# Order of the last products of a sum of squares, and a scheduling priority for the casts of streamed weights, in a two-layer decoder trunk

## The chip, the cores and the metric

The kernel runs on one core of a Trainium2 chip. The metric is the device time in microseconds (us) of one execution; the time of a kernel is the median of several.

## The reference, cut to what matters

The input `h` has 256 tokens of 1024 features, in fp32. Each of two layers adds three sub-layers to it: a SwiGLU feed-forward, a mixer (differential attention, an RWKV-7 recurrence and an HGRN2 recurrence side by side, gated and projected), and a second feed-forward. Each sub-layer begins with a normalization over the features:

```python
def rms_norm(x, w, eps=EPS):
    xf = x.astype(jnp.float32)
    y = xf * lax.rsqrt(jnp.mean(xf * xf, axis=-1, keepdims=True) + eps)
    return (y * w.astype(jnp.float32)).astype(x.dtype)
...
    for l in range(DEPTH):
        ...
        u = modulate(rms_norm(h, norm_w[l, 0]), m[0], m[1])
        h = h + 0.5 * m[2] * swiglu(u, ffn_w_gate[l, 0], ffn_w_up[l, 0], ffn_w_down[l, 0])
        u = modulate(rms_norm(h, norm_w[l, 1]), m[3], m[4])
        ...
        h = h + m[5] * y
        u = modulate(rms_norm(h, norm_w[l, 2]), m[6], m[7])
        h = h + 0.5 * m[8] * swiglu(u, ffn_w_gate[l, 1], ffn_w_up[l, 1], ffn_w_down[l, 1])
```

All weights are fp32 in HBM and each is used once.

## The kernel before

`h` lies transposed on chip as eight tiles of 128 features x 256 tokens. The weights come as a stream of 446 items, each a block of 128 x 1024 fp32 (512 KB, some 384 KB). All but the first six go through `load(i)`: SyncE issues the DMA into `raw` (four buffers), and `split(wh, wl, raw)` (L371 to L373) makes two parts of it, `wh`, a rounded copy made by ScalarE (ACT), and `wl = raw - wh`, made by VectorE (DVE). Each of `wh` and `wl` has three buffers. `mm3` (L369) then multiplies an item with activations that are split in the same way (`uh`, `ul`; `hh`, `hl`; `zh`, `zl`; `yh`, `yl`): three products for each block of 128 x 128, 24 for an item, added up in one of four PSUM banks `psd`. Some mixer items are taken the other way round by `tm_proj` (L953 to L955, products of 512 columns).

The stages follow one another as the items do: in each layer 68 items of the first feed-forward (44 gate and up, 24 down), 87 of the mixer (its last eight, `w_out`, add to `h`) and 68 of the second feed-forward. While the projections of a mixer run on TensorE (PE), the recurrences and the attention are worked through in small pieces between the items: on DVE the inversion of triangular matrices (L800 to L820), and for the attention scores (L1195, L1200 to L1204), exponentials `ae` (L1207 on ACT, L1217 on DVE), their transposes (L1222 on PE, copied to `apt` by L1224 on ACT), the products with the values `av` (L1234; `av` is copied out of its banks by L1174 on ACT), squares of the result `aot` (L1240), its transposes (L1252) and the tiles `oa` for the output projection. Gates `g` leave their banks by L1267 on ACT. L750 is a product of RWKV with a tile `BK` from ACT.

**The normalization.** The last items of a stage (down or `w_out`) each finish one tile of `h`. `z_tile` then makes the split tiles `zh`, `zl` of it and calls `z_square`: ACT squares the tile (L417), and GpSimd (POOL) adds the squares of tiles 1 to 6 to that of tile 0 (`acc`, L419). The square of tile 7 stays by itself as `sq`. `z_sums` sums `acc` and `sq` over the features by PE products with ones (L430, two for each, into one bank `psm`), and a chain of small DVE instructions (`nst`, L434 and L377 to L382) takes the inverse root, from which the diagonal `nv` (L437) and, by one more product (L441), `rstd` is made. `z_sums` is called by `z_close`, after the first item of the next stage has been written, with a priority of 584 (`PRIO["z"]`). The next stage begins with products of `zh`, `zl`, which need no `rstd`, and changes to `uh`, `ul` (made by `make_u`, L392) some items later. There are six such normalizations: one at the start, five at a change of stage.

**What sets the order.** A list scheduler orders the instructions of each engine when the kernel is built: of those that it holds ready, that with the highest priority goes first, and priority falls with the place in the program. `ahead(n)` gives the instructions written under it the priority of a place n instructions earlier. On the chip each engine then runs its list in that order, and waits where an operand or a buffer is not ready.

Of the kernel before, what the change touches and what calls it, by code (L numbers as in the profile page):

```python
# [63 lines left out]
def trunk(ctx: ExitStack, tc: tile.TileContext, A, out):  # L64
# [14 lines left out]
    def psm(shape):  # L79
        return pm.tile(shape, F32, name="psm", tag="psm")  # L80
# [176 lines left out]
    NOW = {}  # L257
# [8 lines left out]
    def ahead(n):  # L266
        return tc.high_priority(n) if n else nullcontext()
# [103 lines left out]
    def split(dst_h, dst_l, src):  # L371
        SC.copy(dst_h, src)  # L372
        V.tensor_sub(dst_l, src, dst_h.bitcast(F32))  # L373


    def rsqrt_few(y, v, t):
        V.tensor_scalar(y.bitcast(I32), v.bitcast(I32), 1, None, ALU.logical_shift_right)  # L377
        V.tensor_scalar(y.bitcast(I32), y.bitcast(I32), -1.0, float(0x5F3759DF), ALU.mult, ALU.add)
        for _ in range(3):
            V.scalar_tensor_tensor(t, v, -0.5, y, ALU.mult, ALU.mult)  # L380
            V.tensor_mul(t, t, y)
            V.scalar_tensor_tensor(y, t, 1.5, y, ALU.add, ALU.mult)  # L382
# [39 lines left out]
    def z_close():  # L422
        with ahead(PRIO["z"]):
            z_sums()

    def z_sums():
        ps = psm([128, 2])
        for i, sq in enumerate((NOW["acc"], NOW["sq"])):
            for b in range(2):
                PE.matmul(ps[:, b:b + 1], sq[:, b * 128:(b + 1) * 128], ones[:, 0:1],  # L430
                          start=i + b == 0, stop=i + b == 2)
        st = NOW["st"] = tp.tile([128, 3, 2], F32, name="nst", tag="nst", bufs=1)
        dg = NOW["dg"] = tp.tile([128, 2, 128], F32, name="nv", tag="nv", bufs=1)
        V.tensor_scalar(st[:, 0], ps, 1.0 / D, EPS, ALU.mult, ALU.add)  # L434
        rsqrt_few(st[:, 1], st[:, 0], st[:, 2])
        for b in range(2):
            V.tensor_scalar(dg[:, b], ident, st[:, 1, b:b + 1], None, ALU.mult)  # L437
# [901 lines left out]
    def load(i):  # L1339
        src, n, fn, b = items[i]  # L1340
        raw = wp.tile([128, n], F32, name="raw", tag="raw", bufs=RAWB)
        nc.sync.dma_start(raw, src)
        wh = wp.tile([128, n], F32R, name="wh", tag="wh", bufs=WHB)
        wl = wp.tile([128, n], F32R, name="wl", tag="wl", bufs=WLB)
        split(wh, wl, raw)
        return wh, wl, fn, b

    live = deque()
# [13 lines left out]
    for t in range(KT):  # L1362
# [7 lines left out]
        if t < NI:  # L1370
            raw = NOW["ff"].tile([128, D], F32, name=f"raw{t}")
# [12 lines left out]
    for i in range(NI, len(items) + AHEAD):  # L1384
        if i < len(items):
            live.append(load(i))
        while len(live) > (AHEAD if i < len(items) else len(items) + AHEAD - 1 - i):
            wh, wl, fn, b = live.popleft()
            advance(b)
            fn(wh, wl)  # L1390
# [80 lines left out]
```

## Time and profile before

| | before |
|---|---|
| median of 3 runs | 1454.53 us (1451.75 to 1456.83) |
| the profiled execution | 1448.06 us, span 1446.4 us |
| PE matmuls busy | 1397.5 us (97%) |
| PE weight loads busy (PEld) | 1325.0 us (92%) |
| DVE busy | 1185.8 us (82%) |
| ACT busy | 804.4 us (56%) |
| POOL busy | 149.0 us (10%) |
| mean granted clock of PE | 0.992 of full speed |

The shares are of the span. PE appears twice: a product first loads 128 x 128 of one operand (PEld), and the matmul proper then streams the other; the two overlap. The profile is of one execution, which was shorter than the median of the three timed ones.

### The profile page before, as it was taken

The numbers are of one execution on the slowest core, as the hardware profiler recorded it, in microseconds if no ns is written. First come the engines' busy times: TensorE is split into PE (matmuls) and PEld (weight loads), VectorE is DVE, ScalarE is ACT, GpSimd is POOL, SyncE is SP. The second block draws the span as 40 slices with busy tenths as digits, with TensorE's granted clock in tenths as the row PEclk, the third lists the DMA queues.
The fourth block names the chain that finished last, engine by engine and source line by source line (L and its number), as shares of the span: only waits on it lengthen the run. The fifth ranks groups of instructions, "written<-read, shape, count | busy, mean of one in ns | idle before, by whom it ended". The sixth has DMA issues, their size and how long they took to land. (4 is left out here: it accounts for less than half of the span.)

```text
span 1446.4 us, 31230 instructions
## 1 busy us (share of the span) xinstructions
PE 1397.5 (97%) x12424; PEld 1325.0 (92%) x12424; DVE 1185.8 (82%) x2216; ACT 804.4 (56%) x1375; POOL 149.0 (10%) x251
## 2 busy tenths in 40 slices
PE   4999999999899999999999999999989999999998
PEld 2899999998778999999999999999877889999998
DVE  5899988869779999888879888787797787886553
ACT  3565457874255646554555554588534664565542
POOL 6100010031310021000100000100322001100000
PEclk9999999999799999999999999999999999999999
DMA  9679985445416657899878998644552235665664
GB/s 334 247 267 359 341 303 167 148 155 163 137 61 191 203 190 265 298 330 319 297 255 292 353 347 294 194 141 142 180 162 83 88 129 175 198 220 194 193 197 124
DMA packets 90212, 315.99 MB, mean 218 GB/s; under 512 B 10577, under 2 KB 13009, under 8 KB 90066
## 3 DMA queue, kind: packets, MB, share of 16 engines
q1 hardware_dynamic: 86690, 308.32, 63.0%
q0 software_dynamic: 1600, 4.20, 1.2%
q8 instruction: 97, 1.59, 0.4%
q10 hardware_dynamic: 1776, 1.48, 0.3%
q14 instruction: 49, 0.40, 0.1%
HBM read 311.86 MB, written 2.10 MB: 217 GB/s over the span
## 5 line engine op out<-in xcount | busy, mean ns | idle before, releaser
L372 ACT CAST wh<-raw 128x1024 fp32r<-128x1024 f32 (+1 forms) x440 | 455.9, 1036 | 427.4 <-PE psd L369 241.5
L373 DVE TENSOR_TENSOR wl<-raw,wh 128x1024 fp32r<-128x1024 f32 (+1 forms) x440 | 537.2, 1222 | 109.1 <-ACT wh L372 106.2
L369 PE MATMUL psd<-uh,wl 128*128 128x256 f32 x1664 | 227.5, 278 | 6.2 <-DVE wl L373 6.2
L369 PE MATMUL psd<-uh,wh 128*128 128x256 f32 x1664 | 230.8, 280 | 0.0
L369 PE MATMUL psd<-ul,wh 128*128 128x256 f32 x1664 | 226.6, 278 | 0.0
L369 PEld LDWEIGHTS psd<-uh,wl 128*128 128x128 f32 x1664 | 206.0, 188 | 7.9 <-DVE wl L373 7.4
L369 PEld LDWEIGHTS psd<-uh,wh 128*128 128x128 f32 x1664 | 207.2, 188 | 5.0 <-issue 2.6
L369 PEld LDWEIGHTS psd<-ul,wh 128*128 128x128 f32 x1664 | 206.0, 188 | 0.4
L321 DVE SCALAR_TENSOR_TENSOR mw<-mw,cbc 128x1024 f32<-128x1024 f32 x134 | 168.0, 1256 | 0.0
L369 PE MATMUL psd<-hl,wh 128*128 128x256 f32 x704 | 96.0, 277 | 0.0
L369 PE MATMUL psd<-hh,wl 128*128 128x256 f32 x704 | 95.9, 277 | 0.0
L369 PE MATMUL psd<-hh,wh 128*128 128x256 f32 x704 | 95.5, 276 | 0.0
L419 POOL TENSOR_TENSOR acc<-acc,sq 128x256 f32<-128x256 f32 x36 | 31.4, 873 | 573.2 <-ACT sq L417 572.9
L369 PEld LDWEIGHTS psd<-hh,wl 128*128 128x128 f32 x704 | 87.2, 188 | 0.0
L369 PEld LDWEIGHTS psd<-hl,wh 128*128 128x128 f32 x704 | 87.2, 188 | 0.0
L369 PEld LDWEIGHTS psd<-hh,wh 128*128 128x128 f32 x704 | 87.0, 188 | 0.0
L954 PE MATMUL psd<-wl,uh 128*128 128x512 f32 x160 | 66.9, 418 | 3.9 <-DVE wl L373 3.8
L955 PE MATMUL psd<-wh,ul 128*128 128x512 f32 x160 | 67.7, 423 | 0.0
L953 PE MATMUL psd<-wh,uh 128*128 128x512 f32 x160 | 66.4, 416 | 0.0
L369 PE MATMUL psd<-zh,wh 128*128 128x258 f32 x448 | 65.2, 286 | 0.0
L369 PE MATMUL psd<-zh,wl 128*128 128x258 f32 x448 | 64.9, 283 | 0.0
L369 PE MATMUL psd<-zl,wh 128*128 128x258 f32 x448 | 64.0, 283 | 0.0
(430 smaller groups left out, 2032.0 us busy)
## 6 DMA issues: line engine op xcount, KB each, us to landing
raw<-in_gu SPq DMA_DIRECT2D x176, 512.0 KB, 4.7
mw<-in_modw SPq DMA_DIRECT2D x134, 512.0 KB, 5.4
raw<-in_wfm SPq DMA_DIRECT2D x94, 512.0 KB, 3.3
raw<-in_dn SPq DMA_DIRECT2D x64, 512.0 KB, 4.6
raw<-in_wtm SPq DMA_DIRECT2D x40, 512.0 KB, 3.3
raw<-in_dn SPq DMA_DIRECT2D x32, 384.0 KB, 4.1
raw<-in_wo SPq DMA_DIRECT2D x24, 512.0 KB, 3.3
raw<-in_wout SPq DMA_DIRECT2D x16, 512.0 KB, 3.3
```

The costliest lines, as they stand in the source:

```text
L321: ins = V.scalar_tensor_tensor(w, w, 1.0, NOW["cbc"], ALU.mult, ALU.mult, accum_out=modd[:, l, j, f:f + 1])
L369: PE.matmul(p, w[:, sl[k]], xs[k][x], start=first and i == 0, stop=last and i == 3 * n - 1)
L372: SC.copy(dst_h, src)
L373: V.tensor_sub(dst_l, src, dst_h.bitcast(F32))
L419: GP.tensor_add(NOW["acc"], NOW["acc"], sq)
L953: PE.matmul(ps[b], u[k][0][:, ts_], w1, start=k == 0, stop=False)
L954: PE.matmul(ps[b], u[k][0][:, ts_], w2, start=False, stop=False)
L955: PE.matmul(ps[b], u[k][1][:, ts_], w1, start=False, stop=k == KT - 1)
```

## The change

`z_sums` takes the square of the last tile first and the accumulated squares second; `start` and `stop` go by the place in the loop, so the sum is the same. And the two instructions of `split` in `load` are written under `ahead(100)`. From there on every line number is one higher.

```diff
     def z_sums():
         ps = psm([128, 2])
-        for i, sq in enumerate((NOW["acc"], NOW["sq"])):
+        for i, sq in enumerate((NOW["sq"], NOW["acc"])):
             for b in range(2):
                 PE.matmul(ps[:, b:b + 1], sq[:, b * 128:(b + 1) * 128], ones[:, 0:1],
                           start=i + b == 0, stop=i + b == 2)
...
         wh = wp.tile([128, n], F32R, name="wh", tag="wh", bufs=WHB)
         wl = wp.tile([128, n], F32R, name="wl", tag="wl", bufs=WLB)
-        split(wh, wl, raw)
+        with ahead(100):
+            split(wh, wl, raw)
         return wh, wl, fn, b
```

PE at the end of the first mixer, where `w_out` products (`yh`, `yl`) give way to those of the second feed-forward (`zh`, `zl`):

```order
@@ -2832,5 +2838,4 @@
 L369 MATMUL psd<-yl_6721,wh 128x256
 L369 MATMUL psd<-yl_6746,wh 128x256
-L430 MATMUL psm<-ones,acc 128x1 x2
 L369 MATMUL psd<-yl_6765,wh 128x256
 L369 MATMUL psd<-yh_6613,wl 128x256
@@ -2845,4 +2850,5 @@
 L369 MATMUL psd<-zh,wl 128x258 x6
 L430 MATMUL psm<-ones,sq 128x1 x2
+L430 MATMUL psm<-ones,acc 128x1 x2
 L369 MATMUL psd<-zh,wl 128x258
 L369 MATMUL psd<-zl,wh 128x258 x7
```

The two products of `acc` stood in the last `w_out` item, 22 products of weights ahead of those of `sq`; now they stand right behind them. The same happens at all five changes of stage, with 62 to 64 products between the two places where a feed-forward ends.

DVE in the inversion of the first mixer (`TM` and `Y` are its tiles):

```order
 L800 TENSOR_TENSOR TM<-Y,NT 128x392
 L802 TENSOR_REDUCE Y<-TM 128x2x14
+L373 TENSOR_TENSOR wl<-raw,wh 128x1024
 L800 TENSOR_TENSOR TM<-Y,NT 128x450
-L373 TENSOR_TENSOR wl<-raw,wh 128x1024
 L802 TENSOR_REDUCE Y<-TM 128x2x15
 L373 TENSOR_TENSOR wl<-raw,wh 128x1024
```

One `wl` goes ahead of one L800. From the next L802 to the end of the inversion (L809, L812, L814, L817 with a `wl` behind each) DVE's list is the same in both kernels.

ACT in the attention of the second layer, where the most instructions change places:

```order
 L1207 ACTIVATE ae,ast_15161<-psm,ast_15161,ars_14626 128x256 x2
+L372 CAST wh<-raw 128x1024
+L1224 COPY apt<-psm 128x512
+L372 CAST wh<-raw 128x1024 x2
+L1240 ACTIVATE aot,hss<-psm 128x128 x4
+L1224 COPY apt<-psm 128x512
 L1174 COPY av<-psd 128x512
 L372 CAST wh<-raw 128x1024
-L1224 COPY apt<-psm 128x512
-L1267 ACTIVATE g_14671<-psd 128x256
-L1224 COPY apt<-psm 128x512
-L372 CAST wh<-raw 128x1024
```

Three casts, one copy of `apt` and the squares of `aot` now stand ahead of the second copy of `apt` and the second of `av`. In the rest of the attention and of RWKV a small instruction mostly has one cast more ahead of it than before. On PE the matching small products have moved both ways, by up to 20 products of weights later and, in this attention, the first four L1252 by 20 to 25 earlier; between its first and its second group of L1234 stand 18 products of weights, where there were none.

## Rows read from the trace of the kernel before

**Rows 1.** The page: busy us of each engine, share of span, instructions.

```profile
PE 1397.5 (97%) x12424; PEld 1325.0 (92%) x12424; DVE 1185.8 (82%) x2216; ACT 804.4 (56%) x1375; POOL 149.0 (10%) x251
```

**Rows 2.** PE's waits: what waited, for what, total us, times, longest us.

```profile
PE psd L369 <- DVE wl L373: 6.2, 6, 2.0
PE psm L430 <- POOL acc L419: 5.0, 5, 2.0
PE psd L954 <- DVE wl L373: 3.8, 2, 1.9
...
PE psm L750 <- ACT BK L742: 1.4, 2, 0.7
...
PE psm L1252 <- ACT wh L372: 0.8, 1, 0.8
...
PE psm L1252 <- ACT g L1267: 0.7, 1, 0.7
```

**Rows 3.** PE's timeline at one change of stage: start, us, count, idle before.

```profile
552.32 1.07 PE L369 MATMUL psd<-yh,wh 128*128 128x256 f32 x8
553.23 0.96 PE L369 MATMUL psd<-yl,wh 128*128 128x256 f32 x7
556.22 0.61 PE L430 MATMUL psm<-ones,acc 128*128 128x1 f32 x4 [2.03 <-POOL acc L419]
556.69 0.36 PE L369 MATMUL psd<-yl,wh 128*128 128x256 f32 x1
...
559.42 0.61 PE L430 MATMUL psm<-ones,sq 128*128 128x1 f32 x4
```

**Rows 4.** POOL's timeline at the same place.

```profile
555.44 0.72 POOL L419 TENSOR_TENSOR acc<-acc,sq 128x256 f32<-128x256 f32 x1 [1.67 <-ACT sq L417]
```

**Rows 5.** The first inversion: us, busy (instructions) by engine, PE clock, DMA share, GB/s.

```profile
363.00:367.00 4.00, 2.03 (x17) 1.75 (x15) 4.00 (x3) 0.00 (x0) 1.79 (x3) 1.00 0.20 58
```

**Rows 6.** DVE's timeline in the first inversion.

```profile
364.47 1.28 DVE L373 TENSOR_TENSOR wl<-raw,wh 128x1024 fp32r<-128x1024 f32 x1
365.60 2.35 DVE L817 TENSOR_REDUCE Yh<-TM 128x128 f32<-128x2048 f32 x1
```

**Rows 7.** The same columns as Rows 5, in two longer stretches.

```profile
500.00:600.00 100.00, 97.62 (x830) 96.30 (x829) 90.81 (x181) 56.62 (x93) 13.60 (x15) 1.00 0.71 236
600.00:700.00 100.00, 100.00 (x884) 100.00 (x884) 85.62 (x130) 50.55 (x73) 0.87 (x1) 1.00 0.93 326
```

**Rows 8.** The same columns as Rows 5, where the clock is low.

```profile
367.20:374.00 6.80, 4.92 (x13) 3.81 (x13) 6.74 (x9) 2.73 (x5) 3.97 (x5) 0.50 0.66 211
380.90:391.10 10.20, 10.20 (x174) 8.33 (x172) 3.69 (x7) 2.12 (x4) 1.10 (x2) 0.50 0.27 86
1073.80:1080.60 6.80, 6.10 (x14) 4.79 (x15) 6.61 (x9) 3.29 (x6) 4.96 (x8) 0.50 0.56 174
```

**Rows 9.** DVE's timeline behind the change of stage of Rows 3, up to the last `ul`.

```profile
558.03 0.48 DVE L1303 SCALAR_TENSOR_TENSOR h<-psd,modd,h 128x256 f32<-128x256 f32 x1 [1.58 <-PE psd L369]
...
583.93 0.48 DVE L392 SCALAR_TENSOR_TENSOR ul<-un,mods,uh 128x256 fp32r<-128x256 f32 x1
```

**Rows 10.** PE's timeline behind it: the first product with `ul` there.

```profile
588.96 1.07 PE L369 MATMUL psd<-ul,wh 128*128 128x256 f32 x8
```

**Rows 11.** The page: the two casts, busy us, mean ns, idle before and releaser.

```profile
L372 ACT CAST wh<-raw 128x1024 fp32r<-128x1024 f32 (+1 forms) x440 | 455.9, 1036 | 427.4 <-PE psd L369 241.5
L373 DVE TENSOR_TENSOR wl<-raw,wh 128x1024 fp32r<-128x1024 f32 (+1 forms) x440 | 537.2, 1222 | 109.1 <-ACT wh L372 106.2
```

**Rows 12.** ACT's timeline in the attention of layer 1.

```profile
1181.25 0.62 ACT L1174 COPY av<-psd 128x512 f32<-128x512 f32 x1
1181.72 1.10 ACT L372 CAST wh<-raw 128x1024 fp32r<-128x1024 f32 x1
1182.67 0.64 ACT L1224 COPY apt<-psm 128x512 f32<-128x512 f32 x1
```

**Rows 13.** PE's timeline at the same place.

```profile
1183.65 2.10 PE L1234 MATMUL psm<-av,apt 128*128 128x128 f32 x16
```

## The prediction

> **What bounds the kernel now.** I read the page first: matmuls are busy for 97% of the span, DVE for 82% and ACT for 56% [rows 1]. So a change can pay only where PE stands still or runs slowly, and an instruction saved elsewhere is worth nothing by itself. Next the list of PE's waits, which says where it stands still [rows 2]. Three groups matter. The largest is PE waiting for `wl`, 6.2 us at L369 and 3.8 us at L954, 10.0 us in eight waits. Then come 5.0 us in five waits of L430 for `acc`, the sums on POOL: one for each change of stage. And there are many small ones where a product of attention or RWKV has been put into PE's list before its operand is there; the three largest make 1.4 + 0.8 + 0.7 = 2.9 us.
>
> The timelines say what lies behind each group. At a change of stage PE does its products without a gap, stands for 2.03 us in front of the products of `acc`, and goes on [rows 3]; POOL had begun its last addition at 555.44 and ended it at 556.16 [rows 4], so PE started as soon as it could. The products of `sq` come at 559.42 with no idle time in front of them. In the inversion it is different: in 4.00 us DVE is busy for 4.00 and PE for 2.03 [rows 5], DVE does a long inversion instruction and a `wl` in turn without a gap [rows 6], and PE gets its `wl` as fast as DVE gets there. Elsewhere PE is without a gap: 100.00 of 100.00 us in the second feed-forward [rows 7]. The granted clock is 1.00, that is 2.4 GHz, in the stretches with the waits for `acc` [rows 7], and 0.50, that is 1.2 GHz, in three stretches of 6.8, 10.2 and 6.8 us, two of which follow the waits of an inversion at once [rows 8].
>
> **Part 1: the products of `acc` go last.** What it removes: at all five changes of stage PE now reaches `acc` only behind `sq`. At the place shown that is 559.42 + 0.47 us, if I take for the two pairs of products the 0.47 us from 556.22 to 556.69 [rows 3]; without the wait PE is there 2.2 us sooner, at about 557.7, and POOL was done at 556.16 [rows 4]. So this wait goes wholly, with 1.5 us to spare, and it is the longest of the five [rows 2]; at the feed-forward ends there are 62 or more products, some 7 us, between the old and the new place. The number of products is the same.
>
> The size: the 5.0 us count from the modelled end of the matmul before. Eight matmuls start from 552.32 to 553.23, one each 0.114 us; the last of the seven behind them started at 553.23 + 6 x 0.114 = 553.91, and the product of `acc` at 556.22, 2.31 us later instead of 0.114 [rows 3]. That is 2.20 us lost where the list says 2.03, 0.17 more. Over five waits the loss is 5.0 + 5 x 0.17 = 5.85 us. I take that; bounds are 5.0 and 5.85.
>
> Does it carry to the end? The last update of `h` waits for PE (1.58 us, at 558.03 [rows 9]), so it moves forward with PE, and so do `zh`, `zl` and `sq`. Behind it the stages are PE's without a gap [rows 7]. What is late next: `nst` needs both sums, and gets them 0.47 us later behind `sq` than before, and `rstd` and `make_u` follow. The last `ul` is done at 583.93 + 0.48 = 584.41 and first used at 588.96 [rows 9, 10], 4.5 us of cover; 0.47 us and even one more cast of 1.22 us [rows 11] ahead of it stay inside. Cost 0.
>
> **Part 2: casts 100 instructions ahead.** In the feed-forwards I cost it at nothing, gain or loss. ACT's casts wait for buffers that PE frees: of the 427.4 us of idle time ahead of them PE ended 241.5 [rows 11]. They already come as early as three buffers allow, and PE has no gap to fill [rows 7].
>
> In the inversion a gain is what the words of the change suggest, 10.0 us of waits [rows 2]. I cost it at 0 too, for two reasons. The list of DVE there is the same but for one `wl` that passes one L800. And the limit is DVE's total work: 4.00 us busy out of 4.00 while PE uses 2.03 [rows 5]. Another order of the same instructions makes `wl` earlier by one instruction at most, then three full buffers stop it, and the inversion ends as late. The bound below is the whole 10.0 us and the slow clock behind it.
>
> In attention and RWKV a small instruction has about one more cast ahead of it: 1.04 us on ACT or 1.22 us on DVE [rows 11]. On PE the waiting products mostly stand later too, by up to 20 products of weights, that is 20 x 0.114 = 2.3 us, which covers that. Where they don't, in the attention of layer 1, the second copy of `av` (at 1181.25 before [rows 12]) now stands behind three casts and two copies of `apt`: 3 x 1.04 + 2 x 0.64 = 4.4 us later, plus the squares. PE's first L1234 can't start before the first `apt`, then come 18 products of weights, 2.05 us, so the second group of L1234, which ran without a wait at 1183.65 [rows 13], comes to about 1186 and waits for something between 0 and 1.5 us. Against that stand the 2.9 us of small waits, some of which shrink. Bounds: all 2.9 us gained, or one DVE cast of 1.22 us lost at each of five places (RWKV and both attentions), 6.1 us. I take 0, in the middle of what rows give.
>
> The Trainium skill speaks against such stalls more strongly: in "TensorE: Matmul & The Clock Gate", Part 1 on the clock gate, it says that the slow clock is the default and that activity releases it. By that rule a wait for `acc` would cost its own length and a slow stretch behind it, and removing it would give more. The trace does not agree at these five waits, as the 1.00 of their stretches shows [rows 7], and agrees behind the inversions [rows 8]; so it adds nothing to Part 1, and by it a new wait in attention could cost more than its length.
>
> **The sum.** -5.85 + 0 + 0 + 0 = -5.85 us. Against the profiled execution of 1448.06 us that is 1442.2 us. That execution was 6.5 us (0.4%) under the median of 1454.53 us; a median moves by the same amount: 1448.7 us, 0.40% less. About 0.3%, 4.4 us, is what a measurement of this kernel can tell from no change, so the gain is hardly above it.
>
> **The rivals.**
>
> Small chains take it back (no change). If the moved casts cost the upper bound of Part 2, 6.1 us, the sum is +0.25: 1454.8 us; with half of it 1451.7. For it speaks that ACT's list in the attention of layer 1 has the late `av`; against it that PE's products mostly moved later as well.
>
> Banks in attention (slower). The second `av` is copied 4.4 us later, and until then it holds one of the four `psd` banks, while the gates behind it hold others. If PE waits for that bank for the whole 4.4 us, and the clock then falls as after an inversion, where 6.8 us at 0.50 [rows 8] lose 3.4 us of work, one such place costs 7.8 us: +1.95 net. It decides from two places, both attentions: +9.75, 1464.3 us; from a total of 10.2 us lost the result is slower than before by over 0.3%. For it: the place has a gap-free list on ACT [rows 12]. Against it: in layer 0 the second copy of `av` moves behind one cast only, and the present waits at L1252 are 0.8 us at most [rows 2].
>
> The inversion is relieved too (faster by more). With the `wl` waits gone, 10.0 us [rows 2], the sum is -15.85: 1438.7 us; with no slow clock either, which loses half of 6.8 + 10.2 + 6.8 us [rows 8], -27.8: 1426.8 us. Against it: the unchanged list of DVE and its full load [rows 5, 6].
>
> The change doesn't do what it says: the wait for `acc` only moves behind `sq`. It would give 1454.5 us. Against it: POOL's end at 556.16 [rows 4], 1.5 us before PE is there.
>
> **How the numbers follow.** Forecast (gain of the five waits, the rest within 2 us): 0.55. Small chains take it back, or the wait moves: 0.25. Banks: 0.10. Inversion relieved: 0.10. The predicted time is that of the first, 1448.7 us, by itself 1446 to 1451. The range goes from 1439, the nearer end of the relieved inversion, to 1457, beyond the upper bound of the small chains and short of the banks at both places: about 0.85 of the chance. Of the forecast's 0.55 four fifths lie beyond 4.4 us, 0.44, and with the inversion's 0.10 faster has 0.54. Same is 0.11 + 0.25 = 0.36. Slower is 0.10.
>
> **What would show it.** Right: no wait of L430 for `acc` in the list, `acc` products directly behind `sq` with no idle time, and about 10 us of waits for `wl` at the same two inversions, with the same slow stretches. Wrong in Part 1: a wait of L430 for POOL at a new time, or of `ul` products at the change from `zh` to `uh`. Wrong in Part 2: more or longer waits at L750, L1222, L1234, L1252, or on ACT's `av` and `g` copies by bank, with a new stretch of low clock; or fewer waits for `wl`.

## The result, and the profile after

The changed kernel takes 1464.51 us (median of 4 runs, 1462.77 to 1466.29) against 1454.74 us before: a ratio of 1.0067, 95% interval 1.0044 to 1.0090, so 9.8 us slower. I had forecast 5.85 us faster, and the time lies above the range. The profiled execution took 1466.29 us.

The page's line of engines and PE's list of waits, after (only the numbers of lines from 1345 on are one higher than before):

```profile
PE 1408.1 (96%) x12424; PEld 1334.2 (91%) x12424; DVE 1193.8 (82%) x2216; ACT 802.6 (55%) x1375; POOL 153.4 (10%) x251
```

```profile
PE psd L369 <- DVE wl L373: 7.0, 6, 2.0
PE psd L954 <- DVE wl L373: 3.4, 2, 1.9
PE psm L842 <- DVE Xa L838: 3.0, 2, 1.8
PE psd L369 <- ACT yh L372: 2.6, 3, 1.2
...
PE psm L874 <- DVE R L867: 1.3, 2, 0.7
...
PE psm L865 <- DVE SV L892: 1.1, 2, 0.6
PE psm L770 <- DVE Za L756: 1.0, 2, 0.5
PE psm L897 <- DVE UV L875: 1.0, 2, 0.5
```

Two things are as forecast: L430 waits for POOL no more (it had 5.0 us in five waits [rows 2]), and the waits for `wl` in the inversions are what they were (10.4 us, 10.0 before). New are R, SV and UV of the RWKV recurrence, each once in each layer, Za (L770) in its pairs, and `yh` ahead of `w_out`. The wait for Xa behind the inversion has grown too (0.3 us before), but over the experiments below it is anything from 0.2 to 3.6 us, and what sets it they don't show. The two profiled spans are 18.0 us apart (1464.4 and 1446.4 us), more than the 9.8 us of the medians. Of these 18.0 us PE was busy for 10.6 [rows 1] with the same 12424 products, so more than half of the difference isn't in waits, but in products that took longer.

PE's timeline at the change of stage of [rows 3], after:

```profile
569.99 0.61 PE L430 MATMUL psm<-ones,sq 128*128 128x1 f32 x4
570.46 0.58 PE L430 MATMUL psm<-ones,acc 128*128 128x1 f32 x4
```

Both pairs of sums run one behind the other without idle time. In this kernel Part 1 did what it said.

Three stretches of low clock are new. One, of 10.2 us at 1096 us, lies behind the second inversion; the kernel with the sums alone (below) has one of 6.8 us at the same place. The other two, one in each layer, are at a place where the clock was full before (us, busy by engine, clock, DMA share, GB/s):

```profile
427.00:431.00 4.00, 3.56 (x9) 2.90 (x10) 0.00 (x0) 2.10 (x7) 0.00 (x0) 0.57 0.11 44
...
1137.00:1141.00 4.00, 3.53 (x28) 2.80 (x24) 0.00 (x0) 2.30 (x6) 0.00 (x0) 0.57 0.32 118
```

Of each 4 us, 3.4 us are at 0.50, that is 1.2 GHz, and the rest at 1.00. These two stand at the end of the recurrence. PE's and then DVE's timeline there, after:

```profile
416.59 0.45 PE L901 MATMUL psm<-Za,SV 128*64 128x64 f32 x8
...
419.61 1.07 PE L369 MATMUL psd<-ul,wh 128*128 128x256 f32 x8
420.52 0.84 PE L369 MATMUL psd<-uh,wl 128*128 128x256 f32 x6
421.91 0.39 PE L865 MATMUL psm<-SV,Za 128*64 128x64 f32 x5 [0.55 <-DVE SV L892]
...
422.52 0.51 PE L369 MATMUL psd<-uh,wl 128*128 128x256 f32 x2
423.68 1.07 PE L874 MATMUL psm<-R,Ys 64*64 64x64 f32 x16 [0.66 <-DVE R L867]
425.26 1.09 PE L897 MATMUL psm<-H,UV 64*64 64x64 f32 x16 [0.51 <-DVE UV L875]
...
427.44 2.07 PE L918 MATMUL psm<-O,hmean 128*128 128x256 f32 x4 [0.47 <-ACT O L902]
...
431.03 1.40 PE L676 MATMUL psm<-hones,lnt 128*128 128x2 f32 x12
```

```profile
418.49 1.22 DVE L373 TENSOR_TENSOR wl<-raw,wh 128x1024 fp32r<-128x1024 f32 x1 [0.91 <-ACT O L902]
419.75 0.43 DVE L891 TENSOR_TENSOR st<-psm,SV 64x256 f32<-64x256 f32 x1
420.20 1.20 DVE L1035 TENSOR_TENSOR hw<-hw,hq 128x512 f32<-128x512 f32 x1
421.43 0.42 DVE L892 TENSOR_TENSOR SV<-st,EC 64x256 f32<-64x256 f32 x1
```

The last step of the recurrence is a chain that goes to and fro between DVE and PE: state (L891), SV (L892), product (L865), R (L867), product (L874), UV (L875), product (L897). A `wl` and an L1035 now stand inside it on DVE, and SV is late. PE waits at three links, for 0.55, 0.66 and 0.51 us, and the short products with the gaps between them are followed by a fall of the clock, in which four products of L918 take 2.07 us.

### The profile page after: what moved, and what is told of

Same layout as the page of the kernel before. It is cut to its first block, busy times and chain, and to the rows that moved or that the text cites. A ratio compares the mean times of both kernels' runs of the same rounds, so it can differ in the third digit from the quotient of the medians.

```text
span 1464.4 us, 31225 instructions
## 1 busy us (share of the span) xinstructions
PE 1408.1 (96%) x12424; PEld 1334.2 (91%) x12424; DVE 1193.8 (82%) x2216; ACT 802.6 (55%) x1375; POOL 153.4 (10%) x251
## 4 chain that ended last, share of the span: by engine, by line
PE 73%; DVE 15%; ACT 5%; issue 3%; DMA 2%; POOL 1%; ACTq 0%; DVEq 0%; POOLq 0%
PE psd L369 63%; DVE wl L373 4%; ACT wh L372 1%; DVE mw L321 1%; PE psd L955 1%; DVE TM L800 1%; PE psd L953 1%; PE psd L954 1%; PE psm L750 1%; DMA h<-in_x 1%; DVE TM L809 1%; DVE TM L814 1%; PE psm L848 0%; PE psm L918 0%; ACT ae L1207 0%
## 5 line engine op out<-in xcount | busy, mean ns | idle before, releaser
L419 POOL TENSOR_TENSOR acc<-acc,sq 128x256 f32<-128x256 f32 x36 | 36.0, 1001 | 571.6 <-ACT sq L417 435.7
L953 PE MATMUL psd<-wh,uh 128*128 128x512 f32 x160 | 66.4, 415 | 0.0
```

What stands on the lines that cost most here:

```text
L419: GP.tensor_add(NOW["acc"], NOW["acc"], sq)
L953: PE.matmul(ps[b], u[k][0][:, ts_], w1, start=k == 0, stop=False)
```

## The experiments

All have the sums in the new order except where it says otherwise. A ratio is against the kernel before, run beside it.

**The two parts apart.** `e1_swap` is the first half of the change alone, `e2_casts` the second half alone.

> Only the order of the two sums is changed, the casts have their old place. Theory M (the loss sits in the mixers, where a cast now stands ahead of an instruction of a recurrence that PE waits for): the five waits for acc go, nothing else changes, -5.85 us against before, 1448 to 1450 us, and no wait of L430 in the list. Theory S (moving the sums behind the last square costs something itself, because rstd comes later): no change or slower, 1454 us or more, with a wait at the change from zh to uh.

> Only the casts get the priority, the sums stand as before. Theory M: the five waits for acc stay (5.0 us), and the loss is that of both parts plus 5.85 us: 9.8 + 5.85 = +15.6 us, about 1470 us. Theory S: the loss comes from the other part, so 1455 to 1460 us.

Measured: sums alone 1446.31 us, ratio 0.9941 (0.9920 to 0.9963), 8.6 us faster; casts alone 1471.38 us, ratio 1.0118 (1.0094 to 1.0142). So the sums are worth their forecast or somewhat more, and by the ratios the casts cost 17 to 18 us. Theory S fell. One part of the expectation failed: with the sums alone L430 still waits once, at the end of the first mixer, now for the square of the last tile from ACT:

```profile
PE psm L430 <- ACT sq L417: 0.7, 1, 0.7
```

Eight of the experiments have this wait, of 0.4 to 1.4 us; the changed kernel and the five others with the sums in the new order don't, and wait for `yh` some 20 us ahead of this place instead. In three of the eight (`e3_ffn`, `e10_end`, `e16_invitems`, with 1.3, 1.4 and 0.9 us) a stretch of 3.4 us of low clock follows it; in the kernel before, no low clock followed the 2.03 us of [rows 3]. The recurrence's end with the sums alone, PE and then DVE:

```profile
408.50 0.45 PE L901 MATMUL psm<-Za,SV 128*64 128x64 f32 x8
...
411.62 0.39 PE L865 MATMUL psm<-SV,Za 128*64 128x64 f32 x5
...
412.23 1.20 PE L369 MATMUL psd<-ul,wh 128*128 128x256 f32 x8
...
413.72 0.50 PE L369 MATMUL psd<-uh,wl 128*128 128x256 f32 x2
414.15 0.67 PE L874 MATMUL psm<-R,Ys 64*64 64x64 f32 x14
414.75 0.85 PE L369 MATMUL psd<-uh,wl 128*128 128x256 f32 x5
...
417.51 1.13 PE L918 MATMUL psm<-O,hmean 128*128 128x256 f32 x4 [0.47 <-ACT O L902]
...
419.65 1.40 PE L676 MATMUL psm<-hones,lnt 128*128 128x2 f32 x12
```

```profile
409.54 0.43 DVE L891 TENSOR_TENSOR st<-psm,SV 64x256 f32<-64x256 f32 x1
410.00 0.42 DVE L892 TENSOR_TENSOR SV<-st,EC 64x256 f32<-64x256 f32 x1
410.72 1.23 DVE L373 TENSOR_TENSOR wl<-raw,wh 128x1024 fp32r<-128x1024 f32 x1 [0.30 <-ACT wh L372]
```

Here `wl` stands behind L892, nothing waits for the chain, and the same four products of L918 take 1.13 us. From that L901 to that L676 PE needs 419.65 - 408.50 = 11.15 us, after the change 431.03 - 416.59 = 14.44 us, with 33 products of weights in between in both: 3.3 us in this layer.

The same products of weights stand at other places, though. With the sums alone 16 of them stand between L901 and the main group of L865, 11 between that and L874, and five ahead of L897, so that PE has work while DVE makes R and UV. After the change it is 30, two and none. SV comes 3.3 us later behind L901 than with the sums alone, of which DVE spends 0.91 us idle ahead of `wl`, 1.22 on it and 1.20 on L1035. The 14 products that moved ahead of L865 cover 1.6 us of that, and are then missing at L874 and L897. L897 waits for what a way from PE to DVE and back takes. Ahead of L874, R (L867) is made only at 423.21, behind an L1037 and an L1079 on DVE.

**Which stage.** The priority by the item's number:

```diff
+        with ahead(0 if 68 <= i % 223 < 155 else 100):   # e3_ffn
+        with ahead(100 if 68 <= i % 223 < 155 else 0):   # e4_mixer
             split(wh, wl, raw)
```

> Both parts, but the casts of the 87 items of each mixer keep their old priority; only those of the feed-forwards are ahead. Theory M: as the sums alone, -5.85 us, 1448 to 1450 us. Rival F (the loss comes from the start and the feed-forwards, where casts pass the products with the modulation weights): it keeps most of the +9.8 us, 1460 us or more.

> Both parts, but only the casts of the mixer items are ahead. Theory M: the whole loss, about 1464 us, with waits of L865, L874, L897 of 0.5 to 0.7 us in both layers and a stretch of low clock behind them. Rival F: near 1449 us.

Measured: feed-forwards only 1448.20 us, ratio 0.9950 (0.9931 to 0.9969); mixers only 1463.31 us, ratio 1.0054 (1.0035 to 1.0073). The whole loss sits in the mixers.

**Which part of a mixer.** The same line with other bounds: items 117 to 119 of 223 (`e10_end`), all but these (`e13_notend`), items 68 to 116 (`e12_early`), items 120 to 154 (`e11_late`).

> The sums in the new order, and the priority for only three items in each mixer (its items 49 to 51), whose casts fall on the last step of the RWKV recurrence; DVE's list there is then that of the changed kernel (a wl between the two updates of the state). Theory E (this one place makes over half of the loss, by 1.7 us of waits in each layer at L865, L874, L897 and a stretch of low clock behind them): +6 to +9 us against the sums alone, 1453 to 1456 us, with a stretch of low clock at 425 and at 1137 us. Rival P (the loss is spread over many small places): the waits alone, +3.4 us or less, 1450 us.

> Both parts, with only those three items of each mixer left at their old priority. Theory E: over half of the 14 to 16 us loss is gone, 1453 to 1457 us, no waits at L865 and L897 and no low clock there. Rival P: 1460 us.

> The sums in the new order, the priority only for the first 49 items of each mixer (projections, pairs of RWKV, the inversion). Theory E: +2 to +5 us against the sums alone, from L750, L770 and L842 and a longer stretch of low clock behind the inversion. A gain in the inversion, the rival of the prediction, would show as less than the 10 us of waits for wl; I expect these unchanged.

> The sums in the new order, the priority only for the last 35 items of each mixer (attention, output projections, w_out). Theory E: +2 to +4 us against the sums alone, from waits at L1110 and for yh at w_out. The prediction's rival of banks held in attention: +4 us or more with waits of PE for a bank, and a stretch of low clock in the attention of layer 1.

Measured, as ratios: end 0.9994 (0.9979 to 1.0009), all but the end 1.0018 (1.0005 to 1.0032), early 0.9999 (0.9983 to 1.0015), late 0.9956 (0.9937 to 0.9974). Against the sums alone (0.9941) that is +7.7 us for three items of each mixer, +8.4 us for the early and +2.2 us for the late ones, together 18.3 us, which is what the full change has against the sums alone (1.0067 - 0.9941 = 0.0126, 18.3 us). Each of these differences is uncertain by some 3 us, so that they agree so closely is chance, and the +2.2 us of the late items are not clear of noise. Taking the end out of the full change gives back 0.0049, 7.1 us. Theory E holds for the place and for the time of `e10_end`, but "over half" was too much: it is two fifths, and 1458.29 us for all but the end lies between the two expectations. The early part costs more than I expected; the late part's number is the expected one. The waits of the end alone:

```profile
PE psm L874 <- DVE R L867: 1.3, 2, 0.7
PE psm L865 <- DVE SV L892: 1.1, 2, 0.6
PE psm L897 <- DVE UV L875: 1.0, 2, 0.5
```

These are the three lines of the changed kernel, made by three items. The stretch measured above, L901 to L676, is 11.14 to 11.17 us long, without low clock, in both layers of before and of all nine experiments in which no cast stands inside the chain (`e14_inv`, below, has other products in it), and 14.2 to 15.3 us in the changed kernel, `e2_casts`, `e4_mixer` and `e5_wh`. With the end alone it is 15.23 us in layer 0 and 12.99 us in layer 1; in layer 1 of that execution the clock didn't fall, so by this one layer 1.85 us are the price of the waits, and the rest, 1.2 to 2.3 us, that of the clock. It fell in nine of these ten layers. Taking the casts out of the chain (`e13_notend`) takes both away.

The late part is small: it has the 2.6 us of waits for `yh`, and no wait of PE for a bank and no low clock in attention.

**The early part divided.** Items 68 to 98 run beside the RWKV pairs, items 99 to 116 beside the inversion.

> The sums in the new order, the priority only for the first 31 items of each mixer, whose casts run beside the pairs of RWKV ahead of the inversion. Theory Q (the early part's loss comes from PE's list in the pairs: waits at L750 and L770, and the two small products L708 and L709 that are no longer neighbours): +3 to +6 us against the sums alone, 1450 to 1452 us. Rival R (it comes from the inversion and the low clock behind it): under 2 us, 1448 us.

> The sums in the new order, the priority only for items 31 to 48 of each mixer, whose casts run beside the inversion. Theory Q: under 2 us against the sums alone, about 1448 us, with the same 10 us of waits for wl. Rival R: +4 to +8 us, 1451 to 1455 us, by waits at L842 or a longer stretch of low clock.

Measured: pairs 1456.57 us, ratio 1.0000 (0.9984 to 1.0015); inversion 1446.24 us, ratio 0.9935 (0.9920 to 0.9951), as fast as the sums alone. The pairs carry all of the early part, more than the 3 to 6 us of theory Q, and the inversion loses and gains nothing; rival R fell. From the first L691 of the pairs to the first L953 behind them PE needs 319.83 - 252.90 = 66.93 us with the sums alone and 324.43 - 254.29 = 70.14 us after the change (rows of both, in that order):

```profile
252.90 0.44 PE L691 MATMUL psm<-ident,KS 128*128 128x128 f32 x2
...
319.83 0.39 PE L953 MATMUL psd<-wh,uh 128*128 128x512 f32 x1
```

```profile
254.29 0.44 PE L691 MATMUL psm<-ident,KS 128*128 128x128 f32 x2
...
324.43 0.39 PE L953 MATMUL psd<-wh,uh 128*128 128x512 f32 x1
```

Over all runs it is 66.9 to 67.5 us in both layers where `wh` of these items has no priority (before and seven experiments) and 69.9 to 71.7 us where it has (the changed kernel and seven experiments): about 3 us in each layer, 6 of the 8.4. In the four longest of these (71.5 to 71.7 us, one layer each of `e4_mixer`, `e5_wh`, `e14_inv` and `e15_pairs`) the clock fell for 3.4 us inside the pairs; in no other pairs did it fall. PE's timeline shows one source that is no wait. With the sums alone, and then after the change:

```profile
266.68 0.48 PE L708 MATMUL psm<-xx,lw 64*128 64x256 f32 x1
266.69 0.48 PE L709 MATMUL psm<-xx,lw 64*128 64x256 f32 x1
...
267.31 1.19 PE L369 MATMUL psd<-uh,wh 128*128 128x256 f32 x8
```

```profile
268.35 0.70 PE L708 MATMUL psm<-xx,lw 64*128 64x256 f32 x2
268.98 0.50 PE L369 MATMUL psd<-uh,wh 128*128 128x256 f32 x2
269.41 0.70 PE L709 MATMUL psm<-xx,lw 64*128 64x256 f32 x2
270.03 0.97 PE L369 MATMUL psd<-uh,wh 128*128 128x256 f32 x6
```

L708 and L709 each use 64 of the 128 rows of the array. As neighbours they start 0.01 us apart, and all four take 0.63 us until the next product of weights. In all eight kernels in which these `wh` have the priority, the scheduler has put two products of weights between them, and the four now take 1.68 us from 268.35 to 270.03, of which two products of weights at 0.114 us are 0.23: 0.8 us more, once in each layer. This agrees with the Trainium skill ("TensorEngine Tiling (Array Packing)", Key Properties), by which tiles of the array work independently and a change of tiling drains the engine. How much of the 0.8 us is the drain, and how much that L708 and L709 no longer run side by side, no run separates. The rest lies at L750 (its 64 products of a layer take 7.1 us until the next instruction, 5.7 to 6.1 before), in waits at L770 (0.5 us in each) and in the products of weights themselves (below).

**Which of the two casts.** Only `wh`, or only `wl`, under the priority:

```diff
-        split(wh, wl, raw)
+        with ahead(100):                                 # e5_wh
+            SC.copy(wh, raw)
+        V.tensor_sub(wl, raw, wh.bitcast(F32))
...
+        SC.copy(wh, raw)                                 # e6_wl
+        with ahead(100):
+            V.tensor_sub(wl, raw, wh.bitcast(F32))
```

> The sums in the new order, the priority only for the cast wh on ACT; wl on DVE keeps its own. DVE's list at the end of the recurrence is then that of the changed kernel all the same (a wl between the two updates), since the scheduler has wh ready sooner. Theory E: the loss of that place, +6 to +8 us against the sums alone, about 1454 to 1456 us. Rival A (the loss comes from ACT, where casts stand ahead of copies out of the banks): the same total, but without waits for SV, R and UV of DVE.

> The sums in the new order, the priority only for wl on DVE. The list at the end of the recurrence is then that of the kernel before, but in the pairs of RWKV wl goes ahead. Theory E: no waits at L865 and L897, +4 to +8 us against the sums alone from the early part and the late part: 1452 to 1457 us. Rival A: within 2 us of the sums alone.

Measured: `wh` alone 1461.50 us, ratio 1.0040 (1.0024 to 1.0057); `wl` alone 1447.68 us, ratio 0.9945 (0.9924 to 0.9966). Both expectations of theory E missed in size: `wh` alone makes four fifths of the loss (0.0099 of 0.0126 against the sums alone), `wl` alone none beyond noise. Yet the waits of `wh` alone are those of DVE's chain, so at this place it isn't rival A:

```profile
PE psm L865 <- DVE SV L892: 1.2, 2, 0.7
```

DVE's list at the end of the recurrence is that of the changed kernel in `e5_wh`, with a `wl` between the two updates, though `wl` has its old priority there. `wl` can't go before its `wh`; with `wh` earlier it is ready earlier, and the scheduler places it into the gap that the recurrence leaves on DVE. For `wl` alone the number of rival A came true (within 2 us of the sums alone). In the pairs, where `wh` alone has the full loss and `wl` alone none, these two runs don't tell a cast that is in the way on ACT from a `wl` that follows it on DVE.

**Other places of the same casts.** `e8_m50` has -50 in place of 100; `e14_inv` is the changed kernel with the inversion and the recurrence raised by the same amount:

```diff
-PRIO = {"z": 584, "pro": -396, "rw": 0, "inv": 0, "hlev": 0, "at": 50, "asm": 462}
+PRIO = {"z": 584, "pro": -396, "rw": 0, "inv": 100, "hlev": 0, "at": 50, "asm": 462}
```

> The sums in the new order, and the casts 50 instructions later instead of earlier. If a cast ahead of a chain that PE waits for is the cost, then moving the casts behind has nothing left to give where they already stood behind, and PE may wait for wl: 1446 to 1452 us. Rival G (a cast in the old place still delays chains, so that the best place is later): below 1444 us.

> The changed kernel, with the priority of the inversion and the recurrence behind it raised by the same 100. The two updates of the state stand ahead of wl again. Theory E: the waits at L865 and L897 and the low clock behind them go, about 7 us less than the changed kernel: 1456 to 1459 us. Rival P: the total stays within 3 us of the changed kernel, 1462 us or more.

Measured: -50 gives 1452.15 us, ratio 0.9978 (0.9960 to 0.9995), slower than the old place of the casts (0.9941) and just above what I expected, and rival G fell; +100 for both gives 1467.82 us, ratio 1.0079 (1.0057 to 1.0101). The second missed theory E's number, and its waits say why:

```profile
PE psm L874 <- DVE R L867: 3.5, 4, 1.1
...
PE psm L883 <- DVE UV L875: 2.1, 2, 1.0
...
PE psm L897 <- DVE UV L875: 1.8, 2, 0.9
```

In the last step of the first layer SV is free of its `wl`, but a `wl` now stands in front of R, an L1035 and an L1037 in front of UV, and PE has no product of weights between L865, L874 and L897; it waits for 1.11 and 0.88 us there. In an earlier step a `wl` stands in front of UV, and L883 waits. The delay moved along the chain, and a fall of the clock behind it stayed in both layers.

## Why the prediction was wrong

**Part 1 was right in the main.** All five waits for `acc` went, and no product waits for `ul`. Measured is -8.6 us (-11.6 to -5.4) for -5.85; by the runs with the inversion's items, 0.9935 (0.9920 to 0.9951), the gain is rather 7 to 12 us. What the further 3 us are stays open. One step was not as I had it: I let `sq` move forward with PE. At the end of the first mixer it is late with the sums alone (0.7 us at L430). And [rows 7] hold only one of the five waits; that the clock was full at the other four too the trace shows. That a slow stretch would follow a wait of any length was my own inference: none followed these five, but the three falls of the clock behind a wait for `sq`, which was shorter than the 2.03 us, show that the length of the one wait does not settle it.

**Part 2, feed-forwards and inversion: right.** `e3_ffn` and `e16_invitems` are as fast as the sums alone. In the inversions the waits for `wl` stayed at 10 us, as DVE's full load said.

**Part 2, "In attention and RWKV": the step that failed.** I priced it at 0 with bounds of -2.9 and +6.1 us; the runs show +17 to +18 us. Three things were wrong in it.

First, I wrote that PE's products stand later by up to 20 products of weights, "which covers that". At the end of the recurrence L865 does stand later, by 14 products. But SV is late by 3.3 us, not by one cast, and the 14 products that cover 1.6 us of it had covered the next links of the same chain. So PE waits at three links (0.55 + 0.66 + 0.51 us), where it waited at none.

Second, a wait there has a price beyond its length. I gave this price, the fall of the clock, to the rival in attention, where the changed kernel has no wait for a bank. At the end of the recurrence it is 1.2 to 2.3 us in each layer in which the clock fell.

Third, I took moved products on PE as free when nothing waits. In the pairs 3 us in each layer went mostly without a wait of PE, at products of 64 rows that lost their neighbours and at small products that now stand singly between those of weights.

The rival "Banks in attention" named 1464.3 us, nearly the measured time, by chance, and was wrong in its cause: the late part costs 2.2 us, if anything, and has no wait for a bank. My upper bound for the term was of casts alone (1.22 us at five places), and so could hold neither the clock nor PE's own order.

The sum of what was measured: -8.6 us for Part 1, +8.4 us pairs, +7.7 us end of the recurrence, +2.2 us late part: +9.7 us, against 9.8; with an uncertainty of some 3 us in each term the agreement is closer than the terms allow to expect. Of the pairs' 8.4 us some 2 us are not placed: the low clock behind the second inversion was 6.8 us in the kernel before and 23.9 us in `e11_late`, in both of which the pairs' casts keep their place.

The best version is the first half alone (1446.31 us), 8.6 us under the kernel before; none of the others is faster than it beyond noise.

## What to carry to other kernels

A priority for work that only fills gaps is paid where a chain goes to and fro between two engines: look up, for each such chain, what the new order puts inside it, and what work is left to the waiting engine between each two links; work that covers a late first link is gone at the next ones. Raising the first of two dependent instructions can move the second as well, with its own priority unchanged. And compare PE's own list: neighbours that use different rows of the array are worth keeping together.

## What the hardware showed that I had not expected

At a granted clock of 1.00 the products of weights have two spacings. In the feed-forwards it is nearly always 0.113 us; in the mixers it changes between this and 0.118 us for tens of us at a time. In kernels with the same lists for the pairs it does so at other places: in the first layer the sums alone have 0.113 us throughout, `e16_invitems` has 0.118 us at the start and at the end. Eight products with the sums alone, and then with the early items' casts ahead, at the same place:

```profile
269.25 1.07 PE L369 MATMUL psd<-uh,wl 128*128 128x256 f32 x8
270.15 1.07 PE L369 MATMUL psd<-uh,wh 128*128 128x256 f32 x8
```

```profile
270.30 1.10 PE L369 MATMUL psd<-uh,wl 128*128 128x256 f32 x8
271.24 1.10 PE L369 MATMUL psd<-uh,wh 128*128 128x256 f32 x8
```

Starts are 0.90 us apart in the one and 0.94 us in the other. Over the 425 products of the pairs this is up to 2 us by itself, and may be a part of the scatter between executions of one kernel; what sets it these runs don't show.
